# A transformer trunk: its opening in two parts of 512 features, with loads in a fixed order on two queues

## The chip, the cores and the metric

The kernel runs on one core of one Trainium2 chip. A core has a matmul engine (TensorE, PE in the profile, with its weight loads as PEld), a vector engine (VectorE, DVE), a scalar engine (ScalarE, ACT), a general engine (GpSimd, POOL) and SyncE (SP), which here only asks for transfers. DMA engines move data between memory (HBM) and the on-chip buffer (SBUF); matmul results stand in PSUM. The metric is the time of one execution in microseconds (us), the median of several runs.

## The reference

What is computed is a trunk of two layers with three sublayers each, on 256 tokens of 1024 features in float32. Each sublayer modulates its input with a scale and a shift that come from one conditioning vector, runs a feed-forward block or a mixer, and ends with a gated residual and a layer norm. The change touches the first sublayer's beginning only: its scale and shift, its input, and its first products.

```python
D_MODEL, SEQ, D_FF = 1024, 256, 2816

def swiglu(u, w_gate, w_up, w_down):
    return (jax.nn.silu(u @ w_gate) * (u @ w_up)) @ w_down

def adaln_sublayer(x, m, f, ln_g, ln_b):
    shift, scale, gate = m[:, None, 0], m[:, None, 1], m[:, None, 2]
    y = f(x * (1 + scale) + shift)
    return layer_norm(DEEPNORM_ALPHA * x + (1 + gate) * y, ln_g, ln_b)

cs = jax.nn.silu(c)
mod = (cs @ mod_w[layer] + mod_b[layer]).reshape(bsz, N_SUB, 3, D_MODEL)
x = adaln_sublayer(x, mod[:, 0], lambda u: 0.5 * swiglu(u, ...), ln_g[layer, 0], ln_b[layer, 0])
```

## The kernel before, in words

Features stand on the 128 partitions for the matmuls: u, the modulated input, is kept turned, as eight groups of 128 features by 256 tokens. Every float32 operand is split into a high part, rounded by ACT (L258), and a low part, the difference, formed by DVE or POOL (L259). A product is three matmuls: high by high, high by low, low by high (`mm3`, L263 to L265).

*The modulation* (`mod_gen`, L185). For each sublayer and each of scale (i = 1), shift (i = 0) and gate (i = 2), DVE runs over eight blocks of 128 rows of `mod_w`, loaded by SP, and adds each row block times a column of silu(c) to a sum of 128x1024 (L218 for the first, L225 for the others). PE then sums over the partitions. For the first sublayer's scale and shift this must be over before anything else; all later ones are spread over the sublayers by `pace`, and the one for the first sublayer's gate ends in the sums L180.

*The opening before.* `run` (L839) computes the whole scale of the first sublayer, then the biases (six loads on ACT's queue, L90), x as one load (L325) and the whole shift. The `mod_w` of scale and shift comes in pieces of two row blocks (1 MB, rows of 4 KB, buffers "w8", three of them), the last two alone (512 KB, buffers "wd", three as well). PE turns x in blocks of 128x128 (L282); warming matmuls (`warm`, L124) and one block's product in place of DVE's (0, 0, 5) stand between. Then `make_u` applies scale and shift to all eight groups (L296 on DVE, L298 on ACT) and splits them.

*The feed-forward sublayer* (`ffn`, L411) goes over 11 chunks of 256 hidden columns. For a chunk it loads gate and up weights (1 MB each, rows of 1 KB, into "w8", L442), splits them, and runs 192 matmuls of 256 tokens (L263 to L265; for chunk 0 with an order of its own, L540, with weights in two halves of 128 columns, L505). silu and product follow on ACT and DVE (L548, L551), then a split of the result h. The down weights (512 KB each, into "wd", L458) are split into "hd"; for the first eight POOL forms the low part. Their products (`down`) stand one chunk behind. `pace` mixes the modulation of the next stages in, and `setup_rest` brings the masks and positions for the later sublayers, one piece per chunk.

A planner puts the instructions of each engine in order: by their place in the program, but one that is ready by its own reckoning may pass one that isn't. `behind` keeps what it encloses after a given instruction on the same engine; that is an order, not a wait for its end. A load waits until its buffer has been let go by the last reader. SP and ACT each ask for transfers on a queue of their own, in order.

## Time and profile before

| | us |
|---|---|
| median of 3 runs | 1206.98 |
| lowest and highest | 1205.5, 1210.03 |
| the profiled execution, its own time | 1209.47 |
| its span in the profile | 1207.7 |
| PE busy in the span | 1131.0 (94%) |
| DVE busy in the span | 917.7 (76%) |
| ACT, POOL busy in the span | 548.5, 259.4 |

Times in the views count from the start of the span; 1.8 us of the execution lie around it. A timeline row gives start, duration, engine, line, operation, result<-inputs and, in brackets, how long the engine stood idle before it and what ended that. Several equal instructions in a row are one row (x16), whose duration runs from the first one's start to the last one's end. A matmul's duration covers its way through the array, so consecutive ones overlap, and their distance is read from the starts.

### The profile page before, as it was taken

To read this page: it belongs to the slowest core of one execution; us is meant where nothing else is said; L and a number is where in the kernel's file an instruction comes from. 1 tells how busy PE (TensorE), PEld (TensorE's weight loads), DVE (VectorE), ACT (ScalarE), POOL (GpSimd) and SP (SyncE) were. 2 spreads that over 40 slices of the span, in tenths; PEclk is the share of its full clock that TensorE was granted. 3 is DMA by queue.
4 is the path that set the end of the run, shared out by engine and by line. 5 is a ranking of instruction groups with operands and counts; after the bars stand their busy time and mean duration, and the time that the engine had idled before them with its cause. 6 is when DMAs were issued, how large, how long until landed. Compare 5 with 4: busy or idle time off the path is not lost.

```text
span 1207.7 us, 19560 instructions
## 1 busy us (share of the span) xinstructions
PE 1131.0 (94%) x7703; PEld 1025.9 (85%) x7703; DVE 917.7 (76%) x1404; ACT 548.5 (45%) x963; POOL 259.4 (21%) x186
## 2 busy tenths in 40 slices
PE   4998999998899998999999999999989998999997
PEld 3887999788787887989999899898988877899995
DVE  6699777698986677878775889767789748866545
ACT  0645444456433445543543543434347656544430
POOL 0631000224731452320000342000122234300001
PEclk9998999999999999999999899999989999999999
DMA  9879998453310576789987488888733335885620
GB/s 354 266 252 342 299 327 299 139 179 119 97 36 5 188 270 218 238 293 320 311 298 248 134 284 283 270 278 298 250 122 102 139 105 190 294 253 185 211 71 35
DMA packets 155333, 259.74 MB, mean 215 GB/s; under 512 B 8813, under 2 KB 117354, under 8 KB 155242
## 3 DMA queue, kind: packets, MB, share of 16 engines
q1 hardware_dynamic: 155050, 258.45, 64.4%
q8 instruction: 60, 0.98, 0.3%
q14 instruction: 31, 0.25, 0.1%
q10 hardware_dynamic: 192, 0.05, 0.0%
HBM read 257.43 MB, written 1.05 MB: 214 GB/s over the span
## 4 chain that ended last, share of the span: by engine, by line
PE 51%; DVE 23%; DMA 13%; issue 5%; ACT 4%; POOL 3%; SPq 0%; POOLq 0%; DVEq 0%; ACTq 0%
PE gu L265 8%; PE gu L263 8%; PE gu L264 8%; PE acc L265 6%; PE acc L264 6%; PE acc L263 6%; DMA wd<-ffn_w_down 5%; DMA wd<-mod_w 4%; DVE macc L225 3%; DMA w<-ffn_w_up 2%; DVE g L259 2%; DVE x L383 1%; POOL hd L259 1%; DMA w<-mod_w 1%; DVE u L259 1%
## 5 line engine op out<-in xcount | busy, mean ns | idle before, releaser
L225 DVE SCALAR_TENSOR_TENSOR macc<-wd,csT,macc 128x1024 f32<-128x1024 f32 x112 | 171.5, 1531 | 28.6 <-DMA wd<-mod_w 28.0
L265 PE MATMUL gu<-uT,g 128*128 128x256 f32 x640 | 181.3, 283 | 1.6 <-DVE g L259 1.6
L263 PE MATMUL gu<-uT,g 128*128 128x256 f32 x640 | 181.2, 283 | 1.3 <-ACT sg L548 1.3
L265 PE MATMUL gu<-uT,u 128*128 128x256 f32 x640 | 181.3, 283 | 1.0 <-DVE u L259 1.0
L263 PE MATMUL gu<-uT,u 128*128 128x256 f32 x640 | 181.2, 283 | 0.0
L264 PE MATMUL gu<-uT,u 128*128 128x256 f32 x640 | 181.1, 283 | 0.0
L264 PE MATMUL gu<-uT,g 128*128 128x256 f32 x640 | 181.1, 283 | 0.0
L258 ACT CAST hd<-wd 128x1024 fp32r<-128x1024 f32 x88 | 92.3, 1049 | 136.8 <-DMA wd<-ffn_w_down 118.8
L263 PE MATMUL acc<-hd,h 128*128 128x512 f32 x352 | 141.5, 402 | 0.5 <-ACT h L258 0.5
L265 PE MATMUL acc<-hd,h 128*128 128x512 f32 x352 | 138.0, 392 | 1.8 <-DVE h L259 1.8
L264 PE MATMUL acc<-hd,h 128*128 128x512 f32 x352 | 138.1, 392 | 0.0
L259 DVE TENSOR_TENSOR g<-w,g 128x1024 fp32r<-128x1024 f32 x86 | 117.0, 1364 | 23.9 <-ACT g L258 23.8
L263 PEld LDWEIGHTS gu<-uT,g 128*128 128x128 f32 x640 | 122.7, 192 | 3.2 <-ACT sg L548 1.8
L265 PEld LDWEIGHTS gu<-uT,g 128*128 128x128 f32 x640 | 122.7, 192 | 2.2 <-DVE g L259 2.2
L264 PEld LDWEIGHTS gu<-uT,g 128*128 128x128 f32 x640 | 122.7, 192 | 1.4
L265 PEld LDWEIGHTS gu<-uT,u 128*128 128x128 f32 x640 | 122.9, 192 | 1.2 <-DVE u L259 1.2
L264 PEld LDWEIGHTS gu<-uT,u 128*128 128x128 f32 x640 | 122.9, 192 | 0.0
L263 PEld LDWEIGHTS gu<-uT,u 128*128 128x128 f32 x640 | 122.9, 192 | 0.0
L259 DVE TENSOR_TENSOR u<-w,u 128x1024 fp32r<-128x1024 f32 x81 | 106.6, 1321 | 20.1 <-ACT u L258 20.0
L259 POOL TENSOR_TENSOR hd<-wd,hd 128x1024 fp32r<-128x1024 f32 x32 | 89.6, 2806 | 137.9 <-ACT hd L258 137.9
L258 ACT CAST u<-w 128x1024 fp32r<-128x1024 f32 (+1 forms) x89 | 91.7, 1038 | 58.1 <-DMA w<-ffn_w_up 44.8
L259 POOL TENSOR_TENSOR hl<-w,hl 128x1024 fp32r<-128x1024 f32 x28 | 72.5, 2602 | 202.0 <-ACT hl L258 201.5
(403 smaller groups left out, 2477.6 us busy)
## 6 DMA issues: line engine op xcount, KB each, us to landing
wd<-mod_w SPq DMA_DIRECT2D x130, 512.0 KB, 4.8
wd<-ffn_w_down SPq DMA_DIRECT2D x88, 512.0 KB, 4.6
w<-ffn_w_gate SPq DMA_DIRECT2D x43, 1024.0 KB, 8.4
w<-ffn_w_up SPq DMA_DIRECT2D x43, 1024.0 KB, 6.3
w<-hyb_w_in SPq DMA_DIRECT2D x16, 1024.0 KB, 6.1
w<-mod_w SPq DMA_DIRECT2D x7, 1024.0 KB, 7.5
w<-hyb_w_out SPq DMA_DIRECT2D x4, 1024.0 KB, 5.0
w<-mla_w_out SPq DMA_DIRECT2D x4, 1024.0 KB, 5.1
```

The lines of the kernel that those rows point to most:

```text
L225: step = nc.vector.scalar_tensor_tensor(acc, w, c, acc, ALU.mult, ALU.add)
L258: i = self.nc.scalar.copy(hi, src)
L259: return i, (eng or self.nc.vector).tensor_tensor(out=lo, in0=src, in1=hi.bitcast(F32), op=ALU.subtract)
L263: nc.tensor.matmul(out, lh, rh, start=first, stop=False)
L264: nc.tensor.matmul(out, lh, rl, start=False, stop=False)
L265: self.last_mm = nc.tensor.matmul(out, ll, rh, start=False, stop=last)
L383: V.tensor_tensor(out=x[:, b, sl], in0=tmp, in1=x[:, b, sl], op=ALU.add)
```

## The change

The opening is done for features 0 to 511 and then for 512 to 1023. For each part the scale's and then the shift's `mod_w` come as two pieces of 512 rows by 512 columns (1 MB, rows of 2 KB) on SP's queue, each kept behind the one ahead of it (`opened`). DVE adds them up in a PSUM bank, 128x512 at a time, with the last result in SBUF (`open`). Four column products on PE give scale or shift for the part's four groups; x is turned, modulated and split for these groups alone.

On ACT's queue stand the bias loads, two instead of six, then the part's half of x (512 KB) and 512 rows of a chunk's gate and up weights (512 KB each, into "wd"): chunk 0's in the first part, chunk 1's in the second (`early`). The second batch is behind the cast of the first. The other 512 rows of both chunks come on SP's queue behind all of the opening's `mod_w` (`load(0, 1)`, `load(1, 1)`, into "w8"), and everything else that SP loads for chunks 0 and 1 stands behind these.

The matmuls of chunk 0 on the first part's features are traced after the first part, those of chunk 1 on the same features after the second, and the rest where the chunks stand in `ffn` (`products`). They are as many as before, three per product. Both parts' low weights come from POOL, except the gate's second halves, which DVE does. Four warming matmuls follow the turning of x in the first part, two the shift's column products in each part; those of before, and the block that PE multiplied in place of DVE, are gone.

```diff
--- before.py
+++ after.py
@@ -85,9 +85,10 @@
         nc, c, t = self.nc, self.const, self.t
         n = 2 * KD
         rows = self.tl(self.wp, [P, P], "tmp", bufs=2)[0 : 6 * n]
-        for si, (l, j) in enumerate(self.subs):
-            src = t["mod_b"][l, 3 * j * D : (3 * j + 2) * D].rearrange("(r p) -> r p", p=P)
-            nc.scalar.dma_start(rows[si * n : (si + 1) * n], src)
+        for l in range(DEPTH):
+            src = t["mod_b"][l].rearrange("(j e) -> j e", j=3)[:, 0 : 2 * D].rearrange("j (r p) -> j r p", p=P)
+            mark = nc.scalar.dma_start(rows[3 * l * n : 3 * (l + 1) * n], src)
+        yield mark
         pt = self.bank("gu")
         nc.tensor.transpose(pt[:, 0 : 6 * n], rows, self.ident[: 6 * n, : 6 * n])
         self.bcol = c.tile([P, 6, 2, KD], F32, name="bcol")
@@ -118,10 +119,11 @@
         self.nc.gpsimd.tensor_scalar(out, a, eps, None, ALU.add)
         return self.nc.gpsimd.tensor_tensor(out=out, in0=out, in1=self.mhalf[:, 0 : a.shape[-1]], op=ALU.pow)

-    def warm(self, a):
+    def warm(self, a, n=1):

         pt = self.bank("gu")
-        self.nc.tensor.matmul(pt[:, 0 : a.shape[-1]], self.ident, a, start=True, stop=True)
+        for _ in range(n):
+            self.nc.tensor.matmul(pt[:, 0 : a.shape[-1]], self.ident, a, start=True, stop=True)

     def preload(self, func, after):

...
@@ -185,28 +172,21 @@
-        self.AB, self.G = {}, {}
-        todo = [(si, i, k) for si in range(len(self.subs)) for i in (1, 0, 2) for k in range(KD)]
-        ws, loaded, G, step = {}, 0, None, None
+        todo = [(si, i, k) for si in range(len(self.subs)) for i in (1, 0, 2) for k in range(KD) if si or i == 2]
+        ws, loaded, G = {}, 0, None
...
-            elif (si, i, k) == (0, 0, 5):
-                self.share = self.mod_cols0(w, c)
-                with self.behind(self.last_col):
-                    for _ in range(2):
-                        self.warm(self.x[:, 0, 0:512])
             else:
-                step = nc.vector.scalar_tensor_tensor(acc, w, c, acc, ALU.mult, ALU.add)
...
+    def open(self, hf, after, first, second):
+
+
+        nc, t = self.nc, self.t
+        cols, ks = slice(hf * 512, hf * 512 + 512), slice(4 * hf, 4 * hf + 4)
+        A, B = self.AB[0]
+        for i in (1, 0):
+            acc, pt = self.open_acc[i][:, cols], self.bank("gu")
+            for q in range(2):
+                if i and not q:
+                    first()
+                r = self.tl(self.wp, [P, 4, 512], "w8", bufs=3)
+                src = t["mod_w"][0, q * 512 : (q + 1) * 512, i * D + hf * 512 : i * D + hf * 512 + 512]
+                with self.behind(*self.opened):
+                    self.opened = [nc.sync.dma_start(r, src.rearrange("(q p) f -> p q f", p=P))]
+                for k in range(4):
+                    c = self.cs[:, 4 * q + k : 4 * q + k + 1]
+                    if q or k:
+                        nc.vector.scalar_tensor_tensor(acc if q and k == 3 else pt, r[:, k], c, pt, ALU.mult, ALU.add)
+                    else:
+                        nc.vector.tensor_scalar_mul(pt, r[:, k], c)
+            if not i:
+                second()
+            pt = pt[:, 0:4]
+            with self.behind(*after):
+                for k in range(4):
+                    mm = nc.tensor.matmul(pt[:, k : k + 1], acc[:, k * P : (k + 1) * P], self.one[:, 0:1], start=True,
+                                          stop=True)
+            if i:
+                nc.vector.scalar_tensor_tensor(A[:, ks], pt, 1.0, self.bcol[:, 0, 1, ks], ALU.add, ALU.add)
+                turned = []
+                for k0 in range(4 * hf, 4 * hf + 4, 2):
+                    px = self.bank("acc", (P, 2, S))
+                    turned.append((k0, px))
+                    with self.behind(*after):
+                        for q in range(2):
+                            for b in range(NB):
+                                nc.tensor.transpose(px[:, q, b * P : (b + 1) * P],
+                                                    self.x[:, b, (k0 + q) * P : (k0 + q + 1) * P], self.ident)
+                if not hf:
+                    self.warm(self.x[:, 0, 0:512], 4)
             else:
+                nc.vector.tensor_tensor(out=B[:, ks], in0=pt, in1=self.bcol[:, 0, 0, ks], op=ALU.add)
+                with self.behind(mm):
+                    self.warm(self.x[:, 0, 0:512], 2)
+        for k0, px in turned:
+            v = self.tl(self.wp, [P, 2, S], "tmp", bufs=2)
+            nc.vector.tensor_scalar(v[:, 0], px[:, 0], A[:, k0 : k0 + 1], B[:, k0 : k0 + 1], ALU.mult, ALU.add)
+            nc.scalar.activation(v[:, 1], px[:, 1], AF.Identity, scale=A[:, k0 + 1 : k0 + 2], bias=B[:, k0 + 1 : k0 + 2])
+            self.marks[1:] = self.split(self.u[:, 0, k0 : k0 + 2], self.u[:, 1, k0 : k0 + 2], v)
...
+    def opening(self, wg, wu, gp):
+
+
+        nc, t = self.nc, self.t
+        self.x = self.tl(self.wp, [P, NB, D], "x")
+        self.open_acc = [self.tl(self.wp, [P, D], "G", bufs=2) for _ in range(2)]
+        self.AB[0] = [self.tl(self.const, [P, KD], n, bufs=3) for n in "AB"]
+        self.u = u = self.tl(self.wp, [P, 2, KD, S], "uT", F32R)
+        hls, pts, seen, self.opened = {}, {}, [], []
+
+        def load(c, hf):
+            if hf:
+                both = self.tl(self.wp, [P, 2, 4, 256], "w8", bufs=3)
+            for g, w in enumerate((wg, wu)):
+                r = both[:, g] if hf else self.tl(self.wp, [P, 4, 256], "wd", bufs=3)
+                src = w[hf * 512 : hf * 512 + 512, c * 256 : (c + 1) * 256]
+                with self.behind(*self.opened if hf else ()):
+                    i = (nc.sync if hf else nc.scalar).dma_start(r, src.rearrange("(k p) f -> p k f", p=P))
+                if hf:
+                    self.opened = [i]
+                hls[c, hf, g] = hl = self.tl(gp, [P, 2, 4, 256], "gu"[g], F32R)
+                seen[:] = self.split(hl[:, 0], hl[:, 1], r, None if hf and not g else nc.gpsimd)[:1]
+
+        def early(hf):
+            cols = slice(hf * 512, hf * 512 + 512)
+            with self.behind(*seen):
+                i = nc.scalar.dma_start(self.x[:, :, cols], t["x"][0][:, cols].rearrange("(b p) d -> p b d", p=P))
+            with self.behind(i):
+                load(hf, 0)
+
+        def products(c, hf):
+            if not hf:
+                pts[c] = [self.bank("gu" if c else "acc", (P, 2, S)) for _ in range(2)]
+            for kp in (0, 2):
+                for q in range(3):
+                    for s in range(2):
+                        for g in range(2):
+                            for k in (kp, kp + 1):
+                                self.last_mm = nc.tensor.matmul(
+                                    pts[c][s][:, g], hls[c, hf, g][:, q // 2, k, s * P : (s + 1) * P], u[:, q % 2, 4 * hf + k],
+                                    start=not (hf or k or q or g), stop=hf == 1 and q == 2 and k == 3, skip_group_check=True)
+
+        bias = self.setup_bias()
+        seen[:] = [next(bias)]
+        self.open(0, (), lambda: [early(0), *bias], lambda: None)
+        products(0, 0)
+        self.open(1, (self.last_mm,), lambda: early(1), lambda: [load(0, 1), load(1, 1)])
+        products(1, 0)
+
+        def rest(c):
+            products(c, 1)
+            return {(s, g): pts[c][s][:, g] for s in range(2) for g in range(2)}
+
+        return rest
...
+                ahead = None
+                part = self.opening(wg, wu, gp)
...
+                with self.behind(*self.opened if c < 2 and not ahead else ()):
+                    tok = c == 0 and ahead is not None
+                    with self.behind(*self.marks if c == 1 and ahead else hm.get(c - 2, ())):
+                        if c > 1 or ahead:
+                            hls = ahead if tok else load(c, False)
+                    if tok:
+                        rows = by_rows(hls)
+                    else:
+                        if c < 2 and not ahead:
+                            pts = part(c)
+                        else:
+                            pts = {(s, g): self.bank("gu", (P, S)) for s in r2 for g in r2}
+                            for s in r2:
+                                for g in r2:
+                                    for k in range(KD):
...
@@ -839,18 +846,14 @@
     def run(self, subs):
         nc = self.nc
         self.subs = subs
-        self.mdone = set()
-        self.count = 0
         self.marks, self.last_mm = [None], None
         self.left = None
         goals = (44, 64, 98, 132, 136, 144)
         self.setup()
-        self.lead = 0
+        self.lead, self.count = 0, 2 * KD
+        self.AB, self.G, self.mdone = {}, {}, {(0, 0), (0, 1)}
         self.bg = self.mod_gen()
-        self.need(0, 1)
-        self.count += next(self.bg)
-        todo = self.todo = [self.sublayer(si, l, j) for si, (l, j) in enumerate(subs)]
-        self.make_u(0, self.x, range(NB))
+        todo = [self.sublayer(si, l, j) for si, (l, j) in enumerate(subs)]
         self.rest = self.setup_rest()
         for si, (l, j) in enumerate(subs):
             last = si == len(subs) - 1
```

## Rows read from the trace of the kernel before

**Rows 1.** The page, part 4: the chain that ended last, by engine.
```profile
PE 51%; DVE 23%; DMA 13%; issue 5%; ACT 4%; POOL 3%; SPq 0%; POOLq 0%; DVEq 0%; ACTq 0%
```

**Rows 2.** Table by stretches: start:end, length, each engine's busy time (instructions), granted clock, DMA.
```profile
32.00:44.40 12.40, 12.40 (x97) 11.67 (x96) 8.54 (x9) 11.47 (x18) 10.72 (x6) 1.00 0.91 296
44.40:63.10 18.70, 17.52 (x124) 16.21 (x123) 12.60 (x17) 8.43 (x13) 7.28 (x5) 1.00 0.75 257
63.10:98.00 34.90, 29.33 (x218) 27.75 (x216) 34.23 (x54) 11.76 (x16) 15.16 (x38) 0.97 0.77 258
98.00:120.00 22.00, 22.00 (x129) 18.64 (x130) 19.89 (x26) 13.45 (x18) 0.00 (x0) 0.89 1.03 357
120.00:220.00 100.00, 100.00 (x722) 94.81 (x721) 74.97 (x95) 41.13 (x58) 0.00 (x0) 1.00 0.90 301
```

**Rows 3.** Timeline of the opening, SP's queue, DVE and PE: start, duration, what.
```profile
1.18 8.24 SPq L202 DMA_DIRECT2D w<-mod_w  x4
6.22 0.75 DVE L218 TENSOR_SCALAR G<-w,csT 128x1024 f32<-128x1024 f32 x1 [3.19 <-DMA w<-mod_w]
26.00 2.61 DVE L225 SCALAR_TENSOR_TENSOR G<-wd,csT,G 128x1024 f32<-128x1024 f32 x2
31.93 0.80 PE L540 MATMUL gu<-uT,g 128*128 128x256 f32 x2
```

**Rows 4.** DMA in 15 to 24, 28.5 to 33.5 and 104 to 107.8 us.
```profile
DMA packets 965, 3.69 MB, mean 411 GB/s; under 512 B 63, under 2 KB 63, under 8 KB 965
q1 hardware_dynamic: 965, 3.69, 102.7%
...
DMA packets 2798, 1.48 MB, mean 296 GB/s; under 512 B 46, under 2 KB 2778, under 8 KB 2798
...
DMA packets 997, 1.36 MB, mean 358 GB/s; under 512 B 26, under 2 KB 878, under 8 KB 997
```

**Rows 5.** Timeline of DVE at 102 us: a PSUM operand of 512 columns, and the next.
```profile
102.73 0.68 DVE L182 SCALAR_TENSOR_TENSOR G<-gu,G 128x512 f32<-128x512 f32 x1
103.33 0.75 DVE L218 TENSOR_SCALAR macc<-wd,csT 128x1024 f32<-128x1024 f32 x1
```

**Rows 6.** Timeline of POOL and DVE at 40 us.
```profile
39.52 5.96 POOL L259 TENSOR_TENSOR hd<-wd,hd 128x1024 fp32r<-128x1024 f32 x2
...
40.58 0.41 DVE L551 TENSOR_TENSOR sg<-gu,sg 128x256 f32<-128x256 f32 x1
41.46 1.75 DVE L259 TENSOR_TENSOR h<-sg,h 128x256 fp32r<-128x256 f32 x1 [0.47 <-ACT h L258]
```

**Rows 7.** Timeline of PE: the end of chunk 1, and a wait in chunk 2.
```profile
57.75 0.28 PE L264 MATMUL gu<-uT,u 128*128 128x256 f32 x1
57.87 0.28 PE L265 MATMUL gu<-uT,u 128*128 128x256 f32 x1
...
63.90 0.38 PE L265 MATMUL gu<-uT,g 128*128 128x256 f32 x1 [0.37 <-DVE g L259]
```

**Rows 8.** Timeline of SP's queue and of POOL at 45 to 55 us, and POOL's down splits to 100 us (ns min/median/max).
```profile
45.87 0.43 SPq L100 DMA_DIRECT2D prow<-ln_g  x1
52.93 0.33 SPq L198 DMA_DIRECT2D wd<-mod_w  x1
...
54.47 0.40 SPq L442 DMA_DIRECT2D w<-ffn_w_gate  x1
...
49.49 5.77 POOL L259 TENSOR_TENSOR hd<-wd,hd 128x1024 fp32r<-128x1024 f32 x2 [4.02 <-ACT hd L258]
...
L259 POOL TENSOR_TENSOR hd<-wd,hd x8: 2417/2934/3436, 39.5 to 93.1; 128x1024 fp32r<-128x1024 f32 x8
```

**Rows 9.** Timeline of PE at the sums of the gate, and the stretch behind them.
```profile
97.92 1.19 PE L180 MATMUL gu<-macc,one 128*128 128x512 f32 x1 [4.18 <-DVE macc L225]
...
98.00:102.00 4.00, 4.00 (x6) 1.82 (x7) 2.54 (x6) 2.76 (x5) 0.00 (x0) 0.50 1.09 373
```

**Rows 10.** Timeline of PE: sixteen column products after standing still, and after work.
```profile
17.02 3.57 PE L147 MATMUL gu<-one,G 128*128 128x1 f32 x16 [14.19 <-DVE G L225]
...
25.01 1.84 PE L147 MATMUL gu<-csT,w 128*128 128x1 f32 x16
```

More of the change, by code (lines that the diff above doesn't have):

```diff
@@ L239, in mod_sums @@
         elif i == 1:
-            if si:
-                self.mod_scale(si, self.mod_cols(acc))
-            else:
-                self.scale = self.mod_cols0(acc, self.one[:, 0:1])
-        else:
-            if not si:
-                with self.behind(step):
-                    self.mod_scale(si, self.scale)
-                    self.nc.vector.tensor_tensor(out=self.AB[0][1], in0=self.share[:, 0:KD], in1=self.bcol[:, 0, 0],
-                                                 op=ALU.add)
+            self.mod_scale(si, self.mod_cols(acc))
+        else:
             self.mod_shift(si, acc)
@@ L301, in make_u @@
-        if joint:
-            pts = [rows(k0) for k0 in range(0, KD, 2)]
-            vs = self.tl(self.wp, [P, 2, 2, W], "macc")
-            self.warm(n[:, 0, 0:512])
-            while self.count < 2 * KD:
-                self.count += next(self.bg)
-            next(self.todo[0])
-            self.need(si, 0)
-            with self.behind(self.last_col):
-                for _ in range(2):
-                    self.warm(n[:, 0, 0:512])
-            for k0 in range(0, KD, 2):
-                with self.behind(self.marks[1]):
-                    affine(k0, pts[k0 // 2])
-                if k0 < 4:
-                    with self.behind(self.marks[1]):
-                        self.marks[1:] = self.between[k0 // 2]()
-        else:
-            for k0 in range(0, KD, 2):
-                affine(k0, rows(k0))
@@ L542, in ffn @@
-                if c == 1 and ahead:
-                    turned(rows)
-                for s in r2:
-                    i = 2 * c + s
-                    if not tok:
-                        sg = self.tl(hp, [P, S], "sg", bufs=2)
-                        nc.scalar.activation(sg, pts[s, 0], AF.Silu)
-                        if i == NT - 1 and f == 0:
-                            self.preload(AF.Tanh, sg)
-                        nc.vector.tensor_tensor(out=sg, in0=pts[s, 1], in1=sg, op=ALU.mult)
-                        h[i] = self.tl(hp, [P, 2, S], "h", F32R, bufs=6)
-                        hm[c] = self.split(h[i][:, 0], h[i][:, 1], sg)
-                        part = hm[c][1]
-                    skip = 3 if first == "start" else 0
-                    after = (self.marks if tok else self.marks[1:]) if c == 0 else ()
-                    with self.behind(*after):
-                        load_down(i)
-                    with self.behind(*[part] if c == 1 else after):
-                        self.pace(max(0, i + 1 - skip) / (NT - 2 - skip))
```

169 lines of the change are left out of this document (56 added, 113 removed).

## The prediction, made before the changed kernel was run

> **What bounds the kernel now.** I read the chain of work first: 51% of it is TensorE (PE), 23% VectorE (DVE), 13% DMA [rows 1]. A change of the opening therefore pays only as far as PE, the larger part, gets its work earlier and keeps it. Then the table by stretches [rows 2]: from 120 to 220 us PE is busy all the time with DMA at 0.90, so whatever PE is ahead at about 100 us it should keep. Between 32 and 98 us it is not alone: PE is idle 1.2 us of 44.4 to 63.1 and 5.6 us of 63.1 to 98, and in the last of these stretches DVE is busy 34.23 of 34.90 us, while it is idle 3.9 and 6.1 us in the two before. So a lead of PE has to get through a stretch in which DVE has no room, though DVE has 10 us of room ahead of it.
>
> Then the opening itself [rows 3]: the first megabyte of `mod_w` is asked for at 1.18 and DVE starts on it at 6.22; the last two accumulations begin at 26.00 and take 2.61; the first product of chunk 0 starts at 31.93. During all that the DMA engines move 411 GB/s at a share above 1 [rows 4], so the opening is a matter of bytes: 8.39 MB of `mod_w` and 1.05 MB of x must come before any product.
>
> **Part by part, the first products.** The new order needs for products on features 0 to 511 only 4.19 MB of `mod_w`, half of x and half of chunk 0's gate and up weights (1.57 MB), 5.77 MB in all. What a load costs: 1.05 MB at 411 GB/s is 2.55 us, so the 5.04 us from 1.18 to 6.22 hold 2.49 of lead, and a stream begun at 1.18 has landed at 3.67 plus bytes by rate. The rate hangs on the length of a row: 411 GB/s with rows of 4 KB (`mod_w` before), 358 with mostly 1 KB (a chunk's weights), 296 with 512 B (chunk 0's weights before) [rows 4]. The new `mod_w` pieces have 2 KB, which no row shows; between 358 and 411 I take 385. That gives 18.7 us for 5.77 MB.
>
> No row shows two queues with large loads at once. If the second batch on ACT's queue (asked for once the first is cast, some 15 us by the same count) costs the first half nothing, 18.7 stands; if it takes half of the rate from about a us later, the 1.2 us that are left then double, 19.9. I take 19.5, with 18 and 21 from the two rates as ends. The Trainium skill's page "DMA: Bandwidth & Descriptors" (Queues, rings and completion order) says that each DMA engine goes round the queues it has work for, packet by packet; by that alone it would be 19.9, and the two queues bring no bandwidth. No row of the kernel before can show it.
>
> DVE then has four operations of 128x512 left on the last piece. One with an operand in PSUM takes 0.68 us, and the next starts 0.60 after it [rows 5]: 2.4, so 21.9. All but four of the 32 also write to PSUM, which no row shows; nearest is that 0.60, which I take, and its double is a rival below. From the last accumulation to the first product the trace has 28.61 to 31.93, 3.3 us, with sixteen column products and a joint affine; the new tail has four column products and two pairs of features, so 1.9 to 3.3, and I take 2.4. First product at 24.3, against 31.93.
>
> **The second half.** It needs 9.44 MB of `mod_w` and x at 385 and 2.10 MB of weights at 358: 30.4, so landed at 34.1 (31.7 and 35.9 with one rate for all). With 2.4 and 2.4 its products start at 38.9 (36 to 41.6). By then PE has to have done the 48 products of chunk 0 and 48 of chunk 1 that need only the first half; one takes 0.12 us [rows 7], so 11.5 us, 24.3 to 35.8, and PE waits 3 us. The other 96 take 11.5 more; their weights land behind `mod_w` (2.10 MB at 358, 40.0 for the last), their low parts are wanted in the third group of products, and I add 0.5: the end of chunk 1 is at 50.9. Before, its last product began at 57.87 and ends at 57.99 [rows 7]. The lead is 7.1 us (3.5 to 9.9).
>
> **What is hidden.** Six bias loads become two on a queue that carried nothing else; they hide under the first pieces of `mod_w`, and uncovered would cost the 0.4 us or so that one issue takes [rows 8]. The warming products lie in PE's wait for the accumulations. What they buy shows in the same sixteen column products: 3.57 us at 17.02, after PE had stood still, and 1.84 at 25.01, after 8 us of work [rows 10]: half the clock. With transposes and six warming products ahead of 24.3 I take full clock; without, 48 products cost at most 5.8 more, of which PE's 3 us wait takes half. Fewer splits go to DVE, more to GpSimd (POOL): three more of about 2.9 us [rows 8], beside accumulations that read one operand from PSUM. Such an operation took its usual 0.41 beside POOL, while one with both inputs in SBUF took 1.75 for 256 columns [rows 6]; so I add nothing.
>
> **What becomes of the lead.** Chunk 2's weights come next. Before, the SyncE queue sent `mod_w` at 52.93 only when POOL had split the third down weight (49.49, two of 5.77) and let its buffer go, and chunk 2's gate weights stood behind it, at 54.47; PE then missed them by 0.37 [rows 7, 8]. Now POOL is no earlier: the last up piece lands at 40.0, cast 41, then four splits of 2.9 us, 52.6. So the loads of chunk 2 must go ahead of those that wait for POOL. Their own buffers are free by about 36.5 and 41. That the planner lets a ready load pass one whose buffer is not free shows in `prow<-ln_g` at 45.87, traced behind both `mod_w` loads and sent ahead of the second [rows 8]; I take it that it does so here. Then PE's lead reaches the sums L180, where PE now waits 4.18 us for DVE [rows 9]; DVE, with 10 us of room before 63 us, can follow, so I leave that wait as it is. I take off 1.6 for one more pair of waits like those there are now (1.2 before 63.1 us, 0.4 at 63.90). The gain is 7.1 - 1.6 = 5.5 us. The profiled execution took 1209.47 (span 1207.7); 1204.0 is that less 5.5, and as it stands 2.49 above the median of the runs, the forecast is 1201.5.
>
> **The rivals.**
> 1. *The lead is lost at chunk 2.* The loads keep their place behind POOL's release; they come 0.3 us earlier and PE stands 6.8 us. Its clock may then fall, as after the 4.18 us wait: 98 to 102 us ran at a granted clock of 0.50, which cost 2 us [rows 9]. Gain 2 to loss 2: about 1206.5, 1204.5 to 1208.5. For it: the order of the trace before. Against: the buffers are free.
> 2. *The wait at L180 goes too.* DVE has 10 us of room and three splits fewer; if its chain runs ahead by more than PE's lead, the 4.18 and the 2 us at half clock go: 5.5 + 6.2 = 11.7, 1195.3 (1192 to 1198.5).
> 3. *Slower: writing to PSUM has a price on DVE.* With p us per accumulation DVE ends at 7 + 32p + 3 (the first piece, the accumulations, and four operations of some 0.7 for the first half's affine step); the second half's products start 2.4 later and end 11.5 after that. At p = 1.2 that is 62.3 instead of 57.99; PE stands long enough ahead of it to lose 2 us to the half clock: loss 6.3, 1213.3 (1209 to 1216). It decides from p = 1.07 on. For it: no row shows a result of DVE in PSUM. Against: 0.68 with an operand there.
> 4. *Chunk 1's early products don't come early.* They are traced behind the second half's sums; if PE takes them in that order they start at 36.6, and the end is 54.4: lead 3.6, gain 2, 1205 (1203 to 1207).
>
> **How the numbers follow.** Forecast 0.42 (own range 1198.5 to 1204.5), rival 1 0.18, rival 2 0.20, rival 3 0.12, rival 4 0.08. A measurement here can tell about 0.5% from no change, 6.0 us: 1200.95 and 1213.0. Faster by more: 0.4 of the forecast's part and all of rival 2, 0.38; slower by more: somewhat over half of rival 3 and a little of rival 1, 0.10; the rest, 0.52, within. The range 1194 to 1209 leaves out rival 3 and a third of rival 2.
>
> **What would show it.** In the changed profile: first product of chunk 0 near 24, an idle stretch of PE of about 3 us before the second half's products near 39, chunk 1's end near 51; accumulations of 128x512 at 0.60 apart; chunk 2's gate weights asked for before 45 us; a wait of some 4 us at L180, near 92. If PE stands before chunk 2 for over 4 us, rival 1 holds; if accumulations are a us or more apart, rival 3. The prediction fails if the two queues together move clearly less than 358 GB/s, or if DVE's full stretch does not begin earlier than 63 us.

## The result, and the profile of the changed kernel

The changed kernel takes 1220.49 us (median of 4, 1218.48 to 1221.83) where the kernel before takes 1207.54 in the same rounds: 1.0105 times as long, interval 1.0085 to 1.0125. The forecast was 1201.5. The profiled execution took 1219.7 with a span of 1217.9, and against the 1207.7 of before that is 10.2 us; the medians differ by 13.

The table by stretches of the changed kernel, the first four stretches of [rows 2] (start:end, length, busy time and instructions of PE, PEld, DVE, ACT and POOL, granted clock, DMA share, GB/s):

```profile
32.00:44.40 12.40, 8.43 (x52) 8.43 (x52) 8.34 (x11) 2.99 (x5) 3.40 (x2) 0.63 0.31 106
44.40:63.10 18.70, 15.25 (x97) 12.97 (x96) 12.92 (x14) 11.04 (x14) 11.27 (x5) 0.82 0.74 254
63.10:98.00 34.90, 34.90 (x250) 32.95 (x249) 25.99 (x47) 15.96 (x24) 14.25 (x7) 1.00 0.89 278
98.00:120.00 22.00, 16.62 (x92) 13.52 (x92) 20.80 (x32) 7.26 (x10) 6.70 (x36) 0.84 0.86 286
```

The loss is in the first two rows. From 32 to 44.4 us PE does 52 instructions at a clock of 0.63 where it did 97 at 1.00, and DMA falls from 0.91 to 0.31. Behind them PE is full to 98 us; from 120 to 220 us it is busy all the time again, with DMA at 0.91, where [rows 2] has 0.90. The fourth row holds the wait at the gate's sums, 5.38 us here (PE's rows below); before it was 4.18 us and ended at 97.92 [rows 9], in the row above. So whatever happened had happened by 63 us.

The timeline of ScalarE (ACT) and its DMA queue (ACTq), from the cast of chunk 0's first weights to the first half's affine (start, duration, line and operation, out<-in, idle time before it and what ended that):

```profile
18.48 1.05 ACT L222 CAST g<-wd 128x1024 fp32r<-128x1024 f32 x1 [5.99 <-DMA wd<-ffn_w_gate]
19.72 1.05 ACT L222 CAST u<-wd 128x1024 fp32r<-128x1024 f32 x1 [0.20 <-DMA wd<-ffn_w_up]
...
21.99 0.37 ACTq L404 DMA_DIRECT2D wd<-ffn_w_up  x1
29.59 1.04 ACT L222 CAST g<-wd 128x1024 fp32r<-128x1024 f32 x1 [8.83 <-DMA wd<-ffn_w_gate]
33.45 1.04 ACT L222 CAST u<-wd 128x1024 fp32r<-128x1024 f32 x1 [2.81 <-DMA wd<-ffn_w_up]
34.40 1.01 ACT L302 ACTIVATE tmp<-acc,B,A 128x256 f32<-128x256 f32 x2
35.31 1.13 ACT L222 CAST uT<-tmp 128x512 fp32r<-128x512 f32 x2
```

The first half's scale and shift were ready at 26.4. ACT's half of the affine (L302) ran at 34.40, because in ACT's order the casts of chunk 1's two early weights stand ahead of it, and the second of these had been asked for only at 21.99 and landed at 33.4. PE, DVE and the loads all stood behind that. The timeline of PE (L425 are the gate and up products, L280 the column sums, L126 the warming products, L106 turns the parameter rows right behind chunk 1, L167 the gate's sums):

```profile
20.03 0.95 PE L280 MATMUL gu<-one,G 128*128 128x1 f32 x8
24.39 1.87 PE L280 MATMUL gu<-one,G 128*128 128x1 f32 x8 [3.41 <-DVE G L272]
...
35.97 0.79 PE L425 MATMUL acc<-uT,g 128*128 128x256 f32 x2 [6.09 <-ACT uT L222]
...
44.30 0.95 PE L280 MATMUL gu<-one,G 128*128 128x1 f32 x8
...
49.42 1.84 PE L280 MATMUL gu<-one,G 128*128 128x1 f32 x8 [3.45 <-DVE G L272]
51.12 3.76 PE L126 MATMUL gu<-x,ident 128*128 128x512 f32 x4
53.89 1.25 PE L425 MATMUL gu<-uT,g 128*128 128x256 f32 x2
...
72.01 0.27 PE L106 MATMUL gu<-ident,prow 128*128 128x128 f32 x1
...
111.65 2.90 PE L167 MATMUL gu<-macc,one 128*128 128x512 f32 x3 [5.38 <-DVE macc L200]
```

The timeline of DVE, and under it the stretches from 33.3 to 40 and from 41.3 to 44.1 us in the columns of the table above:

```profile
28.18 0.76 DVE L272 SCALAR_TENSOR_TENSOR gu<-w,csT,gu 128x512 f32<-128x512 f32 x1
35.95 2.12 DVE L223 TENSOR_TENSOR uT<-tmp,uT 128x512 fp32r<-128x512 f32 x2 [7.01 <-ACT uT L222]
37.99 3.12 DVE L272 SCALAR_TENSOR_TENSOR gu<-w,csT,gu 128x512 f32<-128x512 f32 x4
...
48.52 0.75 DVE L272 SCALAR_TENSOR_TENSOR G<-w,csT,gu 128x512 f32<-128x512 f32 x1
```

```profile
33.30:40.00 6.70, 4.03 (x19) 4.03 (x20) 3.98 (x5) 2.99 (x5) 2.35 (x1) 0.50 0.00 0
41.30:44.10 2.80, 2.80 (x26) 2.80 (x25) 2.80 (x5) 0.00 (x0) 0.00 (x0) 1.00 0.95 356
```

Read it as a chain. The first product is at 35.97, against 31.93 before [rows 3]; PE takes the 48 products of chunk 0 in 8 us, the first part of them at a granted clock of 0.50, that is 1.2 GHz, and the rest, from about 41 us, at full clock. DVE's low half of the affine stands in DVE's order between the second half's accumulations, so these stop from 28.9 to 38.0; the three `w8` buffers stay full and DMA moves nothing from 33.3 to 40. The second half's shift sums are at 49.42. Chunk 1's early products, which need none of it, begin only at 53.89, behind those sums. Chunk 1 ends at 72.0, where it ended at 57.99 [rows 7]: 14.0 us late. The sums of the gate are at 111.65 instead of 97.92 [rows 9], 13.7 late, and 13 us is what the medians show.

### The profile page after: what moved, and what is told of

Same layout as the page of the kernel before. It is cut to its first block, busy times and chain, and to the rows that moved or that the text cites. A ratio compares the mean times of both kernels' runs of the same rounds, so it can differ in the third digit from the quotient of the medians.

```text
span 1217.9 us, 19543 instructions
## 1 busy us (share of the span) xinstructions
PE 1134.5 (93%) x7693; PEld 1026.3 (84%) x7693; DVE 912.4 (75%) x1416; ACT 547.2 (45%) x961; POOL 263.2 (22%) x187
## 4 chain that ended last, share of the span: by engine, by line
PE 56%; DVE 22%; DMA 10%; ACT 4%; issue 4%; POOL 3%; ACTq 0%; SPq 0%; POOLq 0%; DVEq 0%
PE gu L229 9%; PE gu L227 9%; PE gu L228 9%; PE acc L229 7%; PE acc L228 6%; PE acc L227 6%; DMA wd<-mod_w 3%; DVE macc L200 3%; DMA wd<-ffn_w_down 3%; DVE g L223 2%; POOL hd L223 2%; DMA w<-ffn_w_up 2%; DVE x L360 1%; DVE u L223 1%; DMA wd<-ffn_w_gate 1%
## 5 line engine op out<-in xcount | busy, mean ns | idle before, releaser
L200 DVE SCALAR_TENSOR_TENSOR macc<-wd,csT,macc 128x1024 f32<-128x1024 f32 x112 | 164.5, 1468 | 37.0 <-DMA wd<-mod_w 36.4
L227 PE MATMUL gu<-uT,g 128*128 128x256 f32 x624 | 176.6, 283 | 1.5 <-ACT sg L555 1.5
L228 PE MATMUL gu<-uT,u 128*128 128x256 f32 x624 | 176.6, 283 | 0.0
L229 PE MATMUL gu<-uT,g 128*128 128x256 f32 x624 | 176.6, 283 | 0.0
L227 PE MATMUL gu<-uT,u 128*128 128x256 f32 x624 | 176.6, 283 | 0.0
L229 PE MATMUL gu<-uT,u 128*128 128x256 f32 x624 | 176.6, 283 | 0.0
L228 PE MATMUL gu<-uT,g 128*128 128x256 f32 x624 | 176.6, 283 | 0.0
L222 ACT CAST u<-w 128x1024 fp32r<-128x1024 f32 x86 | 89.7, 1048 | 74.0 <-DMA w<-ffn_w_up 62.3
L227 PEld LDWEIGHTS gu<-uT,g 128*128 128x128 f32 x624 | 119.5, 192 | 3.4 <-ACT sg L555 2.0
L228 PEld LDWEIGHTS gu<-uT,g 128*128 128x128 f32 x624 | 119.5, 192 | 1.4
L228 PEld LDWEIGHTS gu<-uT,u 128*128 128x128 f32 x624 | 119.7, 192 | 0.0
L227 PEld LDWEIGHTS gu<-uT,u 128*128 128x128 f32 x624 | 119.7, 192 | 0.0
L229 PEld LDWEIGHTS gu<-uT,u 128*128 128x128 f32 x624 | 119.7, 192 | 0.0
L229 PEld LDWEIGHTS gu<-uT,g 128*128 128x128 f32 x624 | 119.5, 192 | 0.0
L223 DVE TENSOR_TENSOR u<-w,u 128x1024 fp32r<-128x1024 f32 x78 | 99.2, 1274 | 26.6 <-ACT u L222 26.4
```

Source lines behind the costliest of these rows:

```text
L200: nc.vector.scalar_tensor_tensor(acc, w, c, acc, ALU.mult, ALU.add)
L222: i = self.nc.scalar.copy(hi, src)
L223: return i, (eng or self.nc.vector).tensor_tensor(out=lo, in0=src, in1=hi.bitcast(F32), op=ALU.subtract)
L227: nc.tensor.matmul(out, lh, rh, start=first, stop=False)
L228: nc.tensor.matmul(out, lh, rl, start=False, stop=False)
L229: self.last_mm = nc.tensor.matmul(out, ll, rh, start=False, stop=last)
```

## The experiments

Each kernel is timed beside the kernel before on the same chip. Experiments 1 to 4, 5 to 8, 9 and 10, and 11 and 12 are four groups, each with its own time of the kernel before; across groups the differences from that time are compared. Two times of each trace tell where its opening ended: the end of chunk 1's products (the start of the last one and 0.12 us, as in the 57.99 before), and the start of the gate's sums (97.92 before).

| kernel | ratio to before | interval | chunk 1's end | gate sums |
|---|---|---|---|---|
| changed | 1.0105 | 1.0085 to 1.0125 | 72.0 | 111.65 |
| 1 casts behind | 1.0053 | 1.0034 to 1.0073 | 64.5 | 104.72 |
| 2 chunk 1 early | 1.0126 | 1.0094 to 1.0157 | 72.0 | 113.7 |
| 3 both | 1.0077 | 1.0050 to 1.0103 | 64.7 | 106.58 |
| 4 both, no four warming | 1.0054 | 1.0035 to 1.0073 | 64.2 | 105.49 |
| 5 between the sums | 1.0034 | 1.0022 to 1.0045 | 62.5 | 102.5 |
| 6 between, no four warming | 1.0016 | 1.0000 to 1.0031 | 60.5 | 101.4 |
| 7 casts behind, no four warming | 1.0036 | 1.0024 to 1.0048 | 64.0 | 105.1 |
| 8 before, two bias loads | 1.0010 | 0.9993 to 1.0028 | 58.7 | 98.9 |
| 9 products cut in two | 1.0016 | 1.0002 to 1.0031 | 62.3 | 101.5 |
| 10 and later casts | 1.0023 | 1.0009 to 1.0038 | 57.2 | 101.9 |
| 11 and DVE splits | 0.9998 | 0.9982 to 1.0014 | 57.5 | 100.4 |
| 12 and parameters first | 0.9997 | 0.9988 to 1.0007 | 57.1 | 104.8 (other order) |

**1. ACT's casts behind the affine.** In `load`, for chunk 1's first-part weights only:

```diff
-                seen[:] = self.split(hl[:, 0], hl[:, 1], r, None if hf and not g else nc.gpsimd)[:1]
+                with self.behind(*self.marks[1:2] if c and not hf else ()):
+                    seen[:] = self.split(hl[:, 0], hl[:, 1], r, None if hf and not g else nc.gpsimd)[:1]
```

> The changed kernel with one order added: ACT's casts of chunk 1's early weights stand behind the first part's affine step and casts. Theory (ACT's order): in the changed kernel's trace ACT stands in those two casts, waiting for their loads, from 27 to 34.4 us, the affine step is behind them, DVE's low parts behind that, the second part's accumulations behind those, and then SP's buffers. So first products at 28 to 29 us instead of 35.97, the DMA gap at 33 to 40 us gone, chunk 1 ends near 63 instead of 72.0, and the time falls by some 9 us to about 1211. Rival (the second queue's loads are late and slow the first): the order changes nothing, since the weights land as late as before; first products after 34 us, 1218 to 1221.

Measured 1215.15 (1213.01 to 1219.32) beside 1208.73: 6.4 us over before instead of 13, and 4 us above what was expected. The timelines of ACT, PE and DVE in this kernel (L426 the products):

```profile
27.18 1.02 ACT L302 ACTIVATE tmp<-acc,B,A 128x256 f32<-128x256 f32 x2 [6.46 <-DMA x<-x]
28.09 1.12 ACT L222 CAST uT<-tmp 128x512 fp32r<-128x512 f32 x2
29.12 1.05 ACT L222 CAST g<-wd 128x1024 fp32r<-128x1024 f32 x1
32.93 1.05 ACT L222 CAST u<-wd 128x1024 fp32r<-128x1024 f32 x1 [2.77 <-DMA wd<-ffn_w_up]
```

```profile
41.38 1.84 PE L280 MATMUL gu<-one,G 128*128 128x1 f32 x8 [3.45 <-DVE G L272]
43.07 3.76 PE L126 MATMUL gu<-x,ident 128*128 128x512 f32 x4
45.84 1.20 PE L426 MATMUL gu<-uT,g 128*128 128x256 f32 x1
```

```profile
27.45 0.74 DVE L274 TENSOR_SCALAR gu<-w,csT 128x512 f32<-128x512 f32 x1
...
40.48 0.75 DVE L272 SCALAR_TENSOR_TENSOR G<-w,csT,gu 128x512 f32<-128x512 f32 x1
```

The affine comes 7.2 us earlier, the second part's shift sums 8.0, chunk 1's end 7.5. Half of the loss was this order on ACT. What is left can be seen in the PE rows: 3.45 us of waiting, the sums and the warming at half clock, and only then, at 45.84, products that could have run since 38.

**2 and 3. Chunk 1's early products ahead of the second part**, alone and with the edit of experiment 1:

```diff
-        self.open(1, (self.last_mm,), lambda: early(1), lambda: [load(0, 1), load(1, 1)])
+        early(1)
         products(1, 0)
+        self.open(1, (self.last_mm,), lambda: None, lambda: [load(0, 1), load(1, 1)])
```

> The changed kernel with chunk 1's products on the first part's features traced ahead of the second part, nothing else. Theory (PE's order, the prediction's fourth rival): PE stands or warms from 43.98 to 53.89 us with 48 products ready; they move into that gap, chunk 1 ends 5.8 us earlier, near 66, time about 1214.5. Rival (the end of the second part's loads decides, whatever PE does before): these products are done early but the gain is lost to weights that are not there, 1219 to 1221.

> Both orders of the two runs beside it. Theory: the two costs are separate and add up, 9 and 5.8 us: chunk 1 ends near 57, about where the kernel before has it (57.99), time 1205 to 1207. If the wait for ACT was the only cost, as much as the first alone, 1211. If the second queue is what is slow, 1214 or more.

Measured 1223.26 (1222.21 to 1224.53) and 1217.94 (1216.24 to 1218.81): alone no gain, where 1214.5 was expected, and with the casts moved 2.8 us slower than the casts alone, where 1205 to 1207 was. The timelines of DVE in experiment 2, and of DVE and PE in the kernel with both, say why:

```profile
44.33 0.75 DVE L272 SCALAR_TENSOR_TENSOR G<-w,csT,gu 128x512 f32<-128x512 f32 x1
50.07 0.16 DVE L283 SCALAR_TENSOR_TENSOR A<-gu,bcol 128x4 f32<-128x4 f32 x1 [5.00 <-PE gu L280]
```

```profile
33.64 0.75 DVE L274 TENSOR_SCALAR gu<-w,csT 128x512 f32<-128x512 f32 x1 [2.78 <-DMA w<-mod_w]
...
40.62 0.75 DVE L272 SCALAR_TENSOR_TENSOR G<-w,csT,gu 128x512 f32<-128x512 f32 x1
43.07 0.16 DVE L283 SCALAR_TENSOR_TENSOR A<-gu,bcol 128x4 f32<-128x4 f32 x1 [1.71 <-PE gu L280]
```

```profile
42.09 0.95 PE L280 MATMUL gu<-one,G 128*128 128x1 f32 x8
46.41 1.68 PE L280 MATMUL gu<-one,G 128*128 128x1 f32 x8 [3.38 <-DVE G L272]
```

The scale's sums now stand behind 48 products; DVE's A waits for them, and the shift's last accumulations wait behind A in DVE's order. In experiment 2 DVE stands 5.00 us for these sums, its accumulator done. In the kernel with both the shift sums are 5 us later than in experiment 1, which takes back the products' gain. There the products are not all of it. The row at 33.64 is the shift's first accumulation; DVE stands 2.78 us for its piece of `mod_w`, and in DVE's order it is ahead of all but one of the scale's accumulations, where experiment 1 has it behind six. So the scale's accumulator is done at 41.37 instead of 35.88, and the products end at 41.2. By these rows either alone would have held the sums back by some 5 us; no run takes the two apart. A slow second queue, for which the expectation had 1214 or more, is not what the time shows: ACT's last early cast, which waits for that queue, starts at 32.49, against 32.93 in experiment 1.

**4. The same without the four warming products** ahead of the first part's scale sums (`self.warm(self.x[:, 0, 0:512], 4)` removed).

> Both orders, and without the four warming products after the first part's transposes. In the changed kernel's trace the scale's column products start at 20.03 us behind them although their sums are there at 18.3, and DVE stands 2.1 us for the result. Theory (they are in the way): 2 us earlier through the first part, some 1 to 2 us less than both orders alone, about 1204.5. Rival (the clock): without them the first part's products run at half clock, 0.21 us apart all the way; that costs up to 5.8 us where PE has no wait to hide it, 1206 to 1211.

Measured 1214.82 (1213.54 to 1219.10), 3.1 us less than with them; the 1204.5 expected went by that of experiment 3 and missed with it. The timeline of PE:

```profile
18.07 1.86 PE L280 MATMUL gu<-one,G 128*128 128x1 f32 x8 [1.73 <-DVE G L272]
...
27.84 0.90 PE L424 MATMUL acc<-uT,g 128*128 128x256 f32 x2
```

In the changed kernel the sums, whose accumulator was done at 18.3, stood behind the four products until 20.03. Without them they run at 18.07 and still end earlier, although they take 1.86 us instead of 0.95. That is the time of half clock: the changed kernel's sums at 24.39 take 1.87 at a granted clock of 0.50. The profile gives no granted clock under 1.00 for this stretch, though. The rival did not hold: from 27.8 to 33.6 the granted clock is 1.00, and the products follow each other after 0.12 us. Experiments 5 and 6 below, and 1 and 7, are two more such pairs; each gains 1.5 to 1.7 us without the four. No single pair is far outside its intervals, but the three agree. The gate's sums come 1.1 and 1.2 us earlier in two of the pairs, and 0.3 later from 1 to 7.

**5, 6 and 7. The 48 products between the sums.** Experiment 5 is experiment 1 with chunk 1's early products behind the second part's scale sums and ahead of its shift sums; 6 is 5 without the four warming products, 7 is 1 without them.

```diff
             if not i:
                 second()
+                if hf:
+                    between()
+                    after = (self.last_mm,)
...
-        self.open(1, (self.last_mm,), lambda: early(1), lambda: [load(0, 1), load(1, 1)])
-        products(1, 0)
+        self.open(1, (self.last_mm,), lambda: early(1), lambda: [load(0, 1), load(1, 1)],
+                  lambda: products(1, 0))
```

> Keeps the casts behind the first part's affine (as in the run with that order alone, 1215.2 us, chunk 1's end at 64.6 us against 58.0 before) and traces chunk 1's first-part products after the second part's scale sums and x transposes but ahead of its shift sums. Theory (the place of these 48 products on TensorE costs what is left): they fill the stretch from about 38 us, in which TensorE waited 3.45 us for the shift accumulator, 1.84 us of sums and 3.76 us of warming ran at half clock; shift sums at about 44, second-part products at about 49, chunk 1's end near 60.5 (96 products of 0.12 us), time 1208 to 1211 us. Rival (VectorE's accumulations or the loads hold the second part, wherever the 48 products stand): second-part products no earlier than 52 and chunk 1's end at 64 or later, time 1214 to 1216 us.

> As the run before it, and without the four warming products ahead of the scale's sums. Theory (warming products stand in the way of the sums): everything from the first part's shift sums on is 1.5 to 2.5 us earlier, chunk 1's end near 58.5, time 1206 to 1209 us. Rival (they pay for themselves by keeping the clock up): first products at the lower clock for longer, time equal to the run before it or slower.

> The casts behind the first part's affine, and no four warming products; chunk 1's early products stay behind the second part's sums. Theory: the first part's sums come 2 us earlier and VectorE's second-part accumulations with them; chunk 1's end near 62.6 against 64.6, time 1213 us. Rival (the warming pays for itself): 1215 us or more.

Measured 1212.81 (1212.01 to 1214.64), 1211.27 (1208.90 to 1216.49) and 1213.98 (1211.84 to 1215.35), beside 1209.27. The place of the 48 products is worth 2.9 us (from 1 to 5) or 2.7 (from 7 to 6), and the four warming products 1.5 (from 5 to 6). The theories of 5 and 6 hold in kind, and the sizes are 2 us short: chunk 1's end of experiment 6 is at 60.5 where 58.5 was expected, and that of 7 at 64.0 where 62.6 was. (The 61.4 for experiment 6 in the next expectation is the start of what PE does behind chunk 1.)

**8. The two bias loads alone**, in the kernel before.

> The kernel before with the two bias loads of the change in place of its six, and nothing else. Theory: the six loads on ScalarE's queue were not on the path, so no change: within 2 us of the kernel before. Rival: shorter issue on ScalarE's queue brings the opening forward, 1204 us or less.

Measured 1210.72 (1209.37 to 1213.76) beside 1209.27, an interval that holds no change: the bias loads were off the path.

**9 and 10. What is left in front of the second half.** In 9 the 48 products of experiment 6 are cut in two, 24 on each side of the shift sums. In 10 the casts of chunk 1's second-part weights, and the low half of chunk 0's gate weight, also stand behind the second part's affine:

```diff
+                if hf and (c or not g):
+                    i = None if c else nc.scalar.copy(hl[:, 0], r)
+                    late.append((i, hl, r, eng))
+                    continue
...
+        with self.behind(*self.marks[1:]):
+            for i, hl, r, eng in late:
+                if i is None:
+                    self.split(hl[:, 0], hl[:, 1], r, eng)
+                else:
+                    nc.vector.tensor_tensor(out=hl[:, 1], in0=r, in1=hl[:, 0].bitcast(F32), op=ALU.subtract)
```

> As the run with the 48 products between the sums and without the four warming products (1211.3 us, chunk 1's end at 61.4), but the 48 products are cut in two: 24 ahead of the second part's shift sums, 24 behind them in place of its warming. There the shift accumulator was done at 40.69 us and its sums stood behind the products until 42.98. Theory (a sum must not stand behind products): sums at 40.7 to 41.0, second-part products near 45.5 instead of 47.35, chunk 1's end near 59.5, time about 1209 us. Rival (VectorE's in-order low half of a gate weight, which stands ahead of the shift's B and waits for ScalarE's cast until 41.7, and ScalarE's casts ahead of the affine take the gain): second-part products stay at 47 or later, time 1211 us.

> As the run before it, and the casts of chunk 1's second-part weights, with the low half of chunk 0's gate weight, stand behind the second part's affine on ScalarE and VectorE. Theory (every remaining loss is work standing in order ahead of the affine): second-part products near 45, GpSimd's low halves no longer beside VectorE's low halves of the affine (0.65 us each instead of 2.6), chunk 1's end near 57 against 58.0 in the kernel before, time 1206 to 1208 us, so level with the kernel before or 1 to 3 us below it. Rival (the second-part products wait for chunk 1's casts instead, now late): a wait of 1 us or more inside the second-part products, chunk 1's end at 59 or later, time 1210 us.

Measured 1211.93 (1208.89 to 1214.65) and 1212.49 (1209.98 to 1214.44), beside 1209.16. In 9 the sums came at 40.76 as expected, but the next products only at 47.26, behind a 2.47 us wait for ACT. So the rival held: casts on ACT, and low halves on DVE that wait for them, took the gain. In 10 they began at 44.83 without a wait, and chunk 1's last product ended at 57.2, 0.8 us ahead of the kernel before. Still the time did not fall. The timeline of PE in experiment 9, and those of PE, of SyncE's queue and of POOL in experiment 10, with the stretch behind PE's wait:

```profile
47.26 0.79 PE L430 MATMUL acc<-uT,g 128*128 128x256 f32 x2 [2.47 <-ACT uT L222]
```

```profile
63.03 0.30 PE L106 MATMUL gu<-ident,prow 128*128 128x128 f32 x1 [3.62 <-DMA prow<-ln_b]
```

```profile
58.65 0.38 SPq L101 DMA_DIRECT2D prow<-ln_g  x1
...
60.18 0.40 SPq L490 DMA_DIRECT2D w<-ffn_w_gate  x1
```

```profile
49.90 10.63 POOL L223 TENSOR_TENSOR hd<-wd,hd 128x1024 fp32r<-128x1024 f32 x4
```

```profile
63.40:66.70 3.30, 3.30 (x9) 2.52 (x8) 3.30 (x14) 0.00 (x0) 0.43 (x2) 0.52 1.04 351
```

This is the prediction's first rival, hidden until the opening was fast enough to meet it. POOL has four down weights to split, from 49.90 to 60.5; before, it was done with its early ones at 55.3 [rows 8], and the parameter rows went out at 45.87, chunk 2's gate weights at 54.47. Here they go at 58.65 and 60.18, behind `wd` buffers that POOL frees, and PE stands 3.62 us for the parameter rows. Behind this wait the granted clock is 0.52 from 63.4 to 66.7: nine products of 512 columns follow each other after 0.43 us instead of 0.23, which costs another 1.8 us or so. That is 5.4 us together, and the stretch from chunk 1's end to the gate's sums is 44.7 us here against 39.2 in experiment 9. So the 5 us by which chunk 1 ends earlier than there are lost again.

**11 and 12. The release of the `wd` buffers.** In 11 the second and fourth down weights are split on DVE; in 12 the parameter loads are also traced one chunk earlier.

```diff
-                self.split(dl[:, 0], dl[:, 1], r, nc.gpsimd if i < 8 else None)
+                self.split(dl[:, 0], dl[:, 1], r, nc.gpsimd if i < 8 and (ahead or i not in (1, 3)) else None)
```

> As the run before it (1212.5 us, chunk 1's last product at 57.2 against 58.0 in the kernel before, but chunk 2's gate weights asked at 60.2 against 54.5 and the parameter rows at 58.7, for which TensorE waited 3.6 us), with the low halves of the second and fourth down weights on VectorE instead of GpSimd. Theory (the opening is level now, and what is left is GpSimd's row of four low halves of 2.7 us each from 49.9 to 60.5, behind which the three wd buffers come free, the first rival of the prediction): the buffers come free some 3 to 5 us earlier, chunk 2's gate weights are asked near 56, the wait of 3.6 us goes, gate sums near 98 to 99, time 1207 to 1209 us. Rival (VectorE is the engine that fills the stretch, and its own work gets longer by what is given to it): gate sums stay near 102, time 1212 us or more.

> As the run before it, and the loads of the parameter rows (and the masks that follow them) are traced one chunk earlier, so that they stand ahead of the third down weight on the sync queue. Theory: no wait for parameter rows, chunk 2's gate weights asked near 54 to 55, gate sums near 97.5, time 1206 to 1208 us. Rival (order on the queue moves only who waits, the wd buffers still come free one by one): gate sums within 1 us of the run before it, same time.

Measured 1209.32 (1206.20 to 1213.61) and 1210.36 (1208.86 to 1212.12), beside 1210.48: level with the kernel before. From 10 to 11 the ratio falls by 0.0025, 3 us, with intervals that overlap; of these the traces show 1.5 at the gate's sums. Less was moved than expected: the gate weights are asked at 58.94, not 56, and the wait for the parameter rows is still 2.59 us. In 12 that wait is gone, but chunk 2's gate weights are asked at 58.78, hardly earlier, and PE instead stands 2.71 us for ACT's cast of them; the time is the same, as its rival had it, though the gate's sums are not where it put them. No version beat the kernel before by more than the measurement tells. SyncE's queue and PE in experiment 11, and PE in experiment 12:

```profile
58.94 0.40 SPq L490 DMA_DIRECT2D w<-ffn_w_gate  x1
```

```profile
62.35 0.30 PE L106 MATMUL gu<-ident,prow 128*128 128x128 f32 x1 [2.59 <-DMA prow<-ln_b]
```

```profile
66.32 0.39 PE L227 MATMUL gu<-uT,g 128*128 128x256 f32 x1 [2.71 <-ACT g L222]
```

So the loss of 13 us comes apart, along the chain of experiments, into 6.5 for the casts on ACT, 2.9 for the place of the 48 products, 1.5 for the four warming products, and 3.2 for the casts ahead of the second affine and POOL's splits together (2.0 over before in experiment 6, 1.2 under it in 11). These are 14.1, since experiment 11 ends under the kernel before. The last three sizes are each about as large as their uncertainty.

## Why the prediction was wrong

**The bytes were right.** The last of the first half's loads, chunk 0's up weights, was reckoned landed at 19.5; the cast that waited for it started at 19.72. DMA moved 379 GB/s from 3.7 to 12 us and 376 from 12 to 18, where 385 was taken. How the two queues share was neither of the two cases reckoned, as told in the last section. The first half's last load was not late by it; how long ACT stood in the second batch's casts did hang on it.

**First product at 24.3: wrong, 35.97, and this is the step that failed.** It was worked out as accumulations plus a tail of 2.4 us taken from rows of the same operations. Nothing in it asked what else stands in ACT's order. The prediction weighed the second batch on ACT's queue only by its share of the DMA; that the batch also brings two casts, in order, on the engine that does half of the affine was left out. Experiment 1 prices it at 6.5 of the 13 us. Without it and without the four warming products the first product is at 27.84 (experiment 4): the last 3.5 us of the miss are terms of the sum. DVE ended at 23.28 and not 21.9, because its A waits 1.37 us, in order among the accumulations, for the scale's sums; and the tail was 4.6 us, not 2.4, its sums taking 1.87 where 0.95 is the time at full clock. Full clock was counted on because of the warming products. In the changed kernel the clock did not hold: behind 3.41 us in which PE stood still it was 0.50 for the shift's sums at 24.39, and it stayed there, through the two warming products and another 6.09 us of standing still, until about 41. (The sums at 17.02 of [rows 10], which the prediction puts at half the clock, are so by their duration; the profile gives 1.00 there.)

**Second half landed at 34.1: wrong, because the loads stopped.** The stream was reckoned as bytes by rate, with no buffer. Its pieces go through three `w8` buffers that DVE frees, and DVE stood 7.01 us for ACT's cast of uT. With the casts behind, DMA from 32 to 44.4 us is at 0.91 again and the last accumulation ends at 41.2, where the prediction had 36.5. What set that end in experiment 1 was no longer the loads but DVE: it comes to its second half at 27.45 and is then busy until 41.2 but for 0.70 us. Before that it had stood 3.61 us for a load and 2.47 and 1.96 us for PE's sums, waits that the prediction's sum does not have; no run takes them away.

**Chunk 1's early products: rival 4 held**, given 0.08. They were taken in traced order, behind the second half's shift sums. Its price was reckoned at 3.5 us of lead (an end at 54.4 instead of 50.9); experiment 5 gives 2.9. It also had no place in the forecast's sum beside another miss, while here two came together.

**Chunk 2's loads: the step failed too, but cost nothing in the changed kernel.** They did not pass: `mod_w` was asked at 64.60 and the gate weights at 66.08, not before 45. PE was so late that it did not miss them. Experiment 10 shows the price where PE is on time, 3.62 us of waiting, about half of the 6.8 that rival 1 reckoned with, and behind it 1.8 us at half clock, where rival 1 had 2.

**Rival 3 was not it.** The accumulations take 0.75 us and follow each other after 0.66 to 0.79 us where 0.60 was taken: at 32 of them some 3 us, well short of the 1.07 from which it decided. The size was off, the sign of this rival came true by another mechanism. The wait at the gate's sums (rival 2) was 4.2 to 6.8 us in every kernel but the last, where the order is another and 1.70 us are left.

**One bound does not come out.** With the second half's products at 41.6 the lead would be 4.4 us, not the 3.5 given as its low end; nothing hung on it.

**What stays open.** The stretch from chunk 1's end to the gate's sums is 39.2 to 41.9 us in the other kernels, 44.7 in experiment 10 and 42.9 in 11. The rows put the difference down to the loads behind POOL and the half clock that follows the wait; a run that takes only this wait away was not made. Nor was one that holds DVE's order of experiment 1 in experiment 3, or one with a fourth `w8` buffer.

## What to carry to other kernels

When a change brings loads forward, list every instruction that each load drags along, the casts above all, and write for each engine in order what stands ahead of the step on the path: on an engine that runs in order, one cast that waits for a late load holds everything behind it, the accumulations, the buffers and then the DMA. Move independent products into the stretch in which an engine waits, not to the front of a sum that others wait for, and don't put warming products ahead of a sum that is ready. An opening that becomes faster meets the next ring of buffers; look at what frees them before counting the lead as kept.

## What the hardware showed that was not expected

With two queues active, ACT's got far less than half at first. DMA of the changed kernel from 3.7 to 12 us and from 12 to 18 us, queue by queue (q1 SyncE's, q10 ACT's; packets, MB, share of the time of 16 engines):

```profile
q1 hardware_dynamic: 1302, 2.60, 84.9%
q10 hardware_dynamic: 376, 0.55, 19.6%
...
q1 hardware_dynamic: 677, 1.33, 60.6%
q10 hardware_dynamic: 897, 0.93, 45.2%
```

In the first stretch SyncE's queue had several loads of `mod_w` under way, in rows of 2 KB, and moved 3.5 packets for one of ACT's; x, 0.5 MB asked at 4.72, came only at 14. In the second, when ACT's queue carried the weights with rows of 1 KB, it moved more packets than the other and fewer bytes. A round over the queues packet by packet, which the prediction cites from the Trainium skill's page "DMA: Bandwidth & Descriptors" (Queues, rings and completion order), would give equal numbers of packets, if its packets are those that the trace counts; neither stretch shows that. Together the two queues moved no more than one does, 379 and 376 GB/s, against 411 with rows of 4 KB on one queue [rows 4].

The accumulator in PSUM is a small price: 0.75 us per 128x512, spaced 0.66 to 0.79, against 0.68 and 0.60 for an operation with one operand there [rows 5]. And DVE's low halves of the affine took 0.64 us each where POOL stood still (experiment 1, from 28.90) and 2.6 beside POOL's splits (the same kernel, from 46.82), an operation with both inputs in SBUF, as in [rows 6].
